# A two-layer decode step: compression units and conditioning moved ahead of the first norm, queries and keys projected first, the other projections mixed with attention

## The chip, the cores and the metric

The kernel runs on one core of one Trainium2 chip. The metric is the device time of one execution in microseconds (us). The engines are named as in the profile: PE is TensorE (PEld its weight loads), DVE is VectorE, ACT is ScalarE, POOL is GpSimd, and SP is SyncE, whose queue issues nearly all DMAs of this kernel, one after another and in a fixed order.

## The reference, cut to what matters

Two layers run over 256 prompt tokens and 8 sample tokens (264 columns in the kernel). Cut to what the change touches:

```python
def layer(x, c, ...):
    mod = silu(c) @ ada_w + ada_b                  # conditioning: 6 groups of 1024 columns
    sh1, sc1, g1, sh2, sc2, g2 = split(mod, 6)     # groups j = 0..5
    h = rmsnorm(x) * (1 + sc1) + sh1               # the first norm of a layer: groups 0 and 1
    q, kc, vc, ks, vs, kw, vw, gates, z, xbc, dt = split(h @ w_in, ...)
    kcmp = compress(cached pages of K ++ kc)       # 32-token blocks, stride 16, a small MLP with gelu
    vcmp = compress(cached pages of V ++ vc)
    o_cmp, p = compressed_attention(q, kcmp, vcmp)
    idx = top16(p);  o_slc = selected_blocks(q, idx, ks, vs)
    o_win = window_attention(q, kw, vw)
    o_att = sigmoid(gates) * (o_cmp, o_slc, o_win)
    xbc = silu(causal_conv4(xbc));  y = ssd(xbc, dt, state) * silu(z)   # Mamba-2 part
    x = x + g1 * (concat(o_att, rmsnorm(y)) @ w_out)
    h2 = rmsnorm(x) * (1 + sc2) + sh2
    return x + g2 * ((silu(causal_conv3(h2 @ w_gate)) * (h2 @ w_up)) @ w_down)
```

Every product is made in float32 accuracy out of two halves: ACT copies the high half of a weight tile (whi), DVE subtracts it for the low half (wlo), and TensorE adds high times high, high times low and low times high.

## The kernel before

A **projection tile** is one 128-column slice of w_in: a DMA of 512 KB into a staging buffer `st`, the split (whi on ACT, wlo on DVE), 24 matmuls of 264 columns into a `psmm` buffer, and an ACT copy out of it. A layer projects the gates and dt first (tile from in_wgd), then 6 **conv tiles** (x, B and C of the Mamba part: columns 10 to 15 of w_in, each followed by copies into xr, one ACT and three DVE steps on xa, a tanh and one DVE step into xc), then 10 **q/kv tiles** (keys and values 4 to 9, queries 0 to 3, and with 8 of them a fetch of four cached pages each). The 4 z tiles run inside attention.

**Conditioning** is the generator `ada(l, js)`. A group j is four steps; a step loads two tiles of 512 KB (`ada`, at the program's start `cpg`) and multiplies them in 8 matmuls into `psfl` (the trace counts 16 records). After a group come an ACT copy (adam), 2 transposes and a DVE add into `mod`. In the pools of attention two `ada` buffers exist, so one step's pair of tiles can be in flight: the pair's DMAs wait on SP until the matmuls of the step before have read the buffers, and what stands behind them in SP's queue waits too.

**Compression** of the cached pages is 8 units per layer (4 pairs of samples, keys and values). For each pair 16 DMAs bring pages of 128 KB (`cpg`; each needs a page number read from `pt`, the TENSOR_LOAD and ISA rows), the pages are split, and a unit has 48 matmuls of 252 columns into `pso` (weights cwh, cwl from in_cw), a gelu, and small matmuls.

The order of each engine's queue is static. A scheduler of the framework makes it from the program's order and its own durations; instructions issued while an engine's name is in `pinned` keep program order. Before, PINS is empty. Work is mixed by generators: `side` (conditioning) is advanced once a tile, `first` (the units) once a tile (EARLY, SX, SZ and SQ are all 1), and in attention the string SEQ advances S (samples), P (prompt), M (the Mamba part), B (selected blocks), Z (z tiles) and A (conditioning that is left, `fill`) one step a letter. In layer 0 the units run among the projection tiles. In layer 1 units and groups 0 and 1 have been done in the FFN of layer 0, and `rest` (groups 2 and 3 of layer 1) begins in its down-projection.

At the program's start (the last lines of the listing) two conditioning groups, the norm of layer 0 and the first unit come in this order. `together`, `square`, `norm` and `load` are small helpers; nearly all instructions are recorded with the line of one of them (L117), so groups are told apart by tile names.

Of the kernel before, what the change touches and what calls it, by code (L numbers as in the profile page):

```python
# [9 lines left out]
F32 = mybir.dt.float32  # L10
# [9 lines left out]
TP = 256  # L20
# [14 lines left out]
ADA_BUFS = {"cmp": 3, "att": 2, "ffn": 4}  # L35
# [63 lines left out]
CONSTS = _const_array()  # L99


@with_exitstack
def decode_step(ctx, tc, I, O):
# [75 lines left out]
    load(pt, I["pt"])  # L179
    cT = s1()[:, :256].rearrange("p (a b) -> p a b", a=KC)  # L180
# [131 lines left out]
    def ada(l, js, wide=0):  # L312
# [7 lines left out]
        for j in js:  # L320
            acc = fl()[:, :256]
            for kk in range(0, KC, 2):
                two = []
                if wide:
                    t = ph([2, 4, 256], "cpg", wide)
                    two = [(kk, t[:, 0]), (kk + 1, t[:, 1])]
                for k in (kk, kk + 1):
                    name = pools_names[-1]
                    if not wide:
                        t = sb([4, 256], "ada", ADA_BUFS[name[:3]], F32, pools[-2] if name == "attn1" else pools[-1])  # L330
                        two.append((k, t))
# [146 lines left out]
    def layer(l, A, pa, early, done, side, fill):  # L478
# [10 lines left out]
        for _ in range(GAP[l]):  # L489
            next(side, None)  # L490

        pb = begin(f"attn{l}") if early is None else None
# [27 lines left out]
        first = iter(()) if early is None else early()  # L520
# [45 lines left out]
        for m in range(6):  # L566
            if m % SX == 0:
                next(side, None)
            for _ in range(EARLY):
                next(first, None)  # L570
            o = mtile(I["win"][l, 10 + m], h)
            r = sb([291], "xr", 2)
            G.memset(r[:, 0:3], 0.0)
            G.tensor_copy(r[:, 259:291], cst_in[:, m, :])
            S.activation(r[:, 3:259], o[:, :TP], AF.Copy)
            S.activation(r[:, 262:291:4], o[:, TP:T], AF.Copy)
            G.tensor_copy(cout[:, m, :], r[:, 256:291])
            a = sb([288], "xa", 2)
            S.activation(a, r[:, 0:288], AF.Identity, scale=p["convh"][:, m, 0:1], bias=p["convh"][:, m, 4:5])
            for k in range(1, 4):  # L580
                V.scalar_tensor_tensor(a, r[:, k:k + 288], p["convh"][:, m, k:k + 1], a, op0=OP.mult, op1=OP.add)
            t = s1()
            S.activation(t, a, AF.Tanh)
            V.scalar_tensor_tensor(xc[:, m, :], t, 1.0, a, op0=OP.add, op1=OP.mult)
        store(O["conv"][l], cout)
# [19 lines left out]
        for m in list(range(4, 10)) + list(range(4)):  # L605
            if m % SQ == 0:
                next(side, None)
# [21 lines left out]
        run(first)  # L629
        run(side)  # L630
        if pb is None:
            done()
            pb = begin(f"attn{l}")
# [346 lines left out]
        spare = [slot(n, [KC, 128], F32R) for n in ("whi", "wlo")]  # L980
# [190 lines left out]
        pinned.update(PINS)  # L1171
# [94 lines left out]
    for k in range(KC - 1):  # L1266
        square(k)
    for _ in range(3):
        next(shift)
    load(cst, I["consts"])  # L1270
    square(KC - 1)
    run(shift)
    for _ in range(FIRST):
        next(units)
    params(1)
# [26 lines left out]
SEQ = ("ZBPPMASZPZMBMZZASPSZPPPPSPZAMMMBPSPPZMMAPMMBPPMMSAPBMSPMSASPMBZSMPSPMMSPSPMMPSPPPPPMPPPMPPPMSSSPMAMPAPPMMAPPMMSMP",) * 2  # L1302
CYCLE = "PMZSPAMPSMPBMZ"
GAP = (0, 0)
DOWN = 4
PINS = ()
FIRST, EARLY = 1, 1
SX, SZ, SQ = 1, 1, 1
# [126 lines left out]
```

## Time and profile before

| what | value |
|---|---|
| time, median of 3 runs | 1053.06 us (1047.99 to 1053.59) |
| profiled execution | 1040.78 us, its span 1039.0 us |
| busy: PE, DVE, ACT, POOL | 949.7, 650.7, 487.4, 167.8 us |
| share of PE in the span | 91% |
| chain that ended last | PE 76%, DMA 11%, DVE 7%, ACT 3% |
| mean DMA rate | 212 GB/s |

The span is one execution seen by the profiler. The program's parts stand in it as: the start to the first unit (0 to 42.6 us), the projections of layer 0 with the units (to 163.4), its attention (to 311.5), its output projection and FFN (to 593), the norm of layer 1 (to 609.6), its projections (to 670), its attention (to 816) and the rest. The marks are the starts of PE instructions.

### The profile page before, as it was taken

What the parts mean: (1) busy time and instruction counts of PE and PEld (TensorE: products, weight loads), DVE (VectorE), ACT (ScalarE), POOL (GpSimd) and SP (SyncE); (2) the same over time, 40 slices, a digit from 0 to 9 for tenths busy, and PEclk for the clock granted to TensorE, in tenths of its full rate; (3) what the DMA queues carried; (4) which work ended last, traced back from release to release, by engine and by line L of the source; (5) the groups of instructions that cost most, each with busy time, mean ns of one, the idle gap of its engine ahead of it and who ended that gap; (6) DMA issues with size and microseconds to landing.
All of it is one profiled execution on the core that took longest, in us unless ns stands there. A gap on an engine that the chain in (4) does not pass through costs nothing.

```text
span 1039.0 us, 21345 instructions
## 1 busy us (share of the span) xinstructions
PE 949.7 (91%) x7864; PEld 803.7 (77%) x7864; DVE 650.7 (63%) x1429; ACT 487.4 (47%) x1042; POOL 167.8 (16%) x337
## 2 busy tenths in 40 slices
PE   4599998988997998999999989998999799999996
PEld 2368997653585998999999868875447599999995
DVE  1386643867677665676754575485665687777553
ACT  1356543533444555555634344454244366666441
POOL 2000100225221101001101112031421221111110
PEclk9699999999997999999999989997599899999998
DMA  9987488246757786756675578725283835666651
GB/s 357 313 278 266 158 265 292 94 129 225 270 171 254 232 301 216 238 194 220 210 251 174 183 279 301 244 83 158 91 354 96 330 124 182 183 183 183 194 163 42
DMA packets 101258, 220.35 MB, mean 212 GB/s; under 512 B 11682, under 2 KB 54562, under 8 KB 101026
## 3 DMA queue, kind: packets, MB, share of 16 engines
q1 hardware_dynamic: 97058, 205.28, 59.8%
q0 software_dynamic: 3520, 13.17, 3.1%
q8 instruction: 62, 1.02, 0.4%
q10 hardware_dynamic: 576, 0.54, 0.2%
q14 instruction: 42, 0.34, 0.1%
HBM read 204.70 MB, written 14.25 MB: 211 GB/s over the span
## 4 chain that ended last, share of the span: by engine, by line
PE 76%; DMA 11%; DVE 7%; ACT 3%; issue 2%; SPq 1%; POOL 0%; DVEq 0%; ACTq 0%; POOLq 0%
PE psmm L117 40%; PE psat L117 22%; PE pso L117 10%; PE psfl L117 4%; DMA st<-in_cw_dram 3%; DMA ada<-in_ada_dram 3%; DVE wlo L117 2%; DMA cpg<-in_ada_dram 2%; DMA st<-in_wup_dram 1%; DMA page<-in_wst_dram 1%; DVE s L117 1%; SPq L117 1%; ACT whi L117 1%; DVE rs L117 1%; ACT psc L117 1%
## 5 line engine op out<-in xcount | busy, mean ns | idle before, releaser
L117 DVE TENSOR_TENSOR wlo<-st,whi 128x1024 fp32r<-128x1024 f32 (+1 forms) x204 | 232.7, 1142 | 152.6 <-ACT whi L117 149.1
L117 ACT ACTIVATE whi<-st 128x1024 fp32r<-128x1024 f32 (+1 forms) x204 | 201.6, 990 | 217.5 <-PE psmm L117 150.2
L117 PE MATMUL psmm<-hhi,whi 128*128 128x264 f32 x800 | 233.7, 293 | 3.3 <-ACT whi L117 1.4
L117 PE MATMUL psmm<-hhi,wlo 128*128 128x264 f32 x800 | 228.5, 286 | 1.1 <-DVE wlo L117 1.1
L117 PE MATMUL psmm<-hlo,whi 128*128 128x264 f32 x800 | 228.2, 286 | 0.0
L117 PEld LDWEIGHTS psmm<-hhi,whi 128*128 128x128 f32 x800 | 151.4, 189 | 17.0 <-ACT whi L117 5.2
L117 PEld LDWEIGHTS psmm<-hhi,wlo 128*128 128x128 f32 x800 | 150.9, 189 | 5.2 <-DVE wlo L117 2.4
L117 PEld LDWEIGHTS psmm<-hlo,whi 128*128 128x128 f32 x800 | 151.5, 190 | 2.4 <-issue 2.0
L117 PE MATMUL psmm<-act,whi 128*128 128x264 f32 x704 | 128.5, 284 | 0.0
L117 PEld LDWEIGHTS psmm<-act,whi 128*128 128x128 f32 x704 | 108.9, 188 | 1.6 <-issue 1.6
L117 PE MATMUL psat<-hhi,whi 128*128 128x264 f32 x352 | 100.8, 286 | 2.2 <-ACT whi L117 2.2
L117 PE MATMUL psat<-hhi,wlo 128*128 128x264 f32 x352 | 100.5, 286 | 1.0 <-DVE wlo L117 1.0
L117 PE MATMUL psat<-hlo,whi 128*128 128x264 f32 x352 | 100.6, 286 | 0.0
L117 PE MATMUL psmm<-act,wlo 128*128 128x264 f32 x352 | 99.9, 284 | 0.0
L117 PE MATMUL pso<-whi,cwh 128*128 128x252 f32 x256 | 74.8, 292 | 8.7 <-ACT whi L117 8.0
L117 PE MATMUL pso<-wlo,cwh 128*128 128x252 f32 x256 | 74.1, 290 | 1.8 <-DVE wlo L117 1.8
L117 PE MATMUL pso<-whi,cwl 128*128 128x252 f32 x256 | 73.6, 287 | 0.0
L117 PEld LDWEIGHTS psat<-hhi,whi 128*128 128x128 f32 x352 | 67.1, 191 | 2.5 <-ACT whi L117 2.5
L117 POOL COPY fout<-xr 128x26 f32<-128x26 f32 x44 | 28.1, 639 | 247.0 <-ACT xr L117 247.0
L117 PEld LDWEIGHTS psat<-hhi,wlo 128*128 128x128 f32 x352 | 66.7, 190 | 1.2 <-DVE wlo L117 1.2
L117 PEld LDWEIGHTS psat<-hlo,whi 128*128 128x128 f32 x352 | 67.2, 191 | 0.0
L117 PEld LDWEIGHTS psmm<-act,wlo 128*128 128x128 f32 x352 | 66.1, 188 | 0.0
(305 smaller groups left out, 1579.5 us busy)
## 6 DMA issues: line engine op xcount, KB each, us to landing
st<-in_wup_dram SPq DMA_DIRECT2D x88, 512.0 KB, 3.9
ada<-in_ada_dram SPq DMA_DIRECT2D x80, 512.0 KB, 5.2
st<-in_wdn_dram SPq DMA_DIRECT2D x44, 512.0 KB, 3.6
st<-in_win_dram SPq DMA_DIRECT2D x40, 512.0 KB, 4.9
page<-in_slcc_dram SPq DMA_DIRECT2D x128, 128.0 KB, 2.7
cpg<-in_ada_dram SPq DMA_DIRECT2D x16, 512.0 KB, 9.4
st<-in_cw_dram SPq DMA_DIRECT2D x16, 512.0 KB, 5.9
cpg<-in_cmpc_dram SPq DMA_DIRECT2D x64, 128.0 KB, 3.7
```

The source lines that it names most:

```text
L117: ins = f(*a, **k)
```

## The change

- **Start.** The first 129 columns of the constants are loaded at once, the others after the third unit. All 8 units of layer 0 come before its first norm, with one conditioning step (groups 0 and 1) after each, in program order on PE and SP; PE's pin ends after the conditioning, SP's at the fourth q/kv tile. The x tile is loaded after the first unit's pages. Conditioning at the start uses 9 `ada` buffers rather than 4 pairs of `cpg` ones.
- **Projections.** The 10 q/kv tiles follow the gates. The conv tiles become a generator that runs when attention's generators exist: after each conv tile a few steps of P, B and S (strings EARLY). SEQ loses the steps that stand there; its later part is the same. (pp, in the rows below, are the prompt's probabilities of compressed attention, a step of P.)
- **Conditioning.** Layer 0: group 2 at the side of the q/kv tiles, 3 and 4 in attention (before: 2 and 3, then 4). Layer 1: the side gets `rest` and then group 3, which `rest` already holds (groups 2 and 3), so that group is computed twice; group 4 goes to attention (before: `rest` and group 4 at the side).
- The buffers `spare` are taken after the conv tiles. The rest is renaming and removed arguments.

```diff
-ADA_BUFS = {"cmp": 3, "att": 2, "ffn": 4}
+ADA_BUFS = {"cmp": 9, "att": 2, "ffn": 4}
...
+CST0 = CONST_W["one"][0] + 1
...
     load(pt, I["pt"])
+    load(cst[:, :CST0], I["consts"][:, :CST0])
     cT = s1()[:, :256].rearrange("p (a b) -> p a b", a=KC)
...
-    def ada(l, js, wide=0):
+    def ada(l, js):
...
-                if wide:
-                    t = ph([2, 4, 256], "cpg", wide)
-                    two = [(kk, t[:, 0]), (kk + 1, t[:, 1])]
                 for k in (kk, kk + 1):
                     name = pools_names[-1]
-                    if not wide:
-                        t = sb([4, 256], "ada", ADA_BUFS[name[:3]], F32, pools[-2] if name == "attn1" else pools[-1])
-                        two.append((k, t))
-                    load(two[k - kk][1], I["ada"][l, j, k])
+                    t = sb([4, 256], "ada", ADA_BUFS[name[:3]], F32, pools[-2] if name[:4] == "attn" else pools[-1])
+                    load(t, I["ada"][l, j, k])
+                    two.append((k, t))
...
-        for m in range(6):
-            if m % SX == 0:
-                next(side, None)
-            for _ in range(EARLY):
-                next(first, None)
-            o = mtile(I["win"][l, 10 + m], h)
...
+        def convolved():
+
+            for m in range(6):
+                o = mtile(I["win"][l, 10 + m], h)
...
+                yield
+            store(O["conv"][l], cout)
...
         for m in list(range(4, 10)) + list(range(4)):
-            if m % SQ == 0:
-                next(side, None)
-            for _ in range(EARLY):
-                next(first, None)
-            if pb is not None and len(ring) < PAGES:
+            next(side, None)
+            if len(ring) < PAGES:
                 fetch()
             o = mtile(I["win"][l, m], h)
+            if m == 7:
+                pinned.clear()
...
-        pinned.update(PINS)
+        for m, _ in enumerate(convolved()):
+            for c in EARLY[m] if m < 6 else ():
+                next(bg[c], None)
+        spare += [slot(n, [KC, 128], F32R) for n in ("whi", "wlo")]
         for c in SEQ[l]:
             next(bg[c], None)
...
     params(0)
+    params(1)
+    p0 = begin("cmp0")
+    units, shift = compress(0, 1, 4), ada(0, (0, 1))
+    pinned.update(PINS)
+    for i in range(8):
+        next(units)
+        if i == 0:
+            load(x, I["xT"])
+        if i == 2:
+            load(cst[:, CST0:], I["consts"][:, CST0:])
+            for k in range(KC):
+                square(k)
+        next(shift, None)
+    run(shift)
+    pinned.discard("PE")
+    run(units)
+    end(p0)
     pa = begin("att0")
-    A = pools[-1]
-    p0 = begin("cmp0")
-    units = compress(0, 1, 4)
-    load(x, I["xT"])
-    shift = ada(0, (0, 1), 4)
...
-    rest = layer(0, A, pa, lambda: units, lambda: end(p0), ada(0, (2, 3)), [ada(0, (4,))])
+    rest = layer(0, pools[-1], pa, ada(0, (2,)), [ada(0, (3, 4))])
     pa = begin("att1")
-    layer(1, pools[-1], pa, None, lambda: None, chain(rest, ada(1, (4,))), [])
+    layer(1, pools[-1], pa, chain(rest, ada(1, (3,))), [ada(1, (4,))])
...
-SEQ = ("ZBPPMASZPZMBMZZASPSZPPPPSPZAMMMBPSPPZMMAPMMBPPMMSAPBMSPMSASPMBZSMPSPMMSPSPMMPSPPPPPMPPPMPPPMSSSPMAMPAPPMMAPPMMSMP",) * 2
+SEQ = ("ZMAZZMMZZAZZAMMMSPZMMAPMMPPMMSAPMSPMSASPMBZSMPSPMMSPSPMMPSPPPPPMPPPMPPPMSSSPMAMPAPPMMAPPMMSMP",) * 2
...
-PINS = ()
-FIRST, EARLY = 1, 1
-SX, SZ, SQ = 1, 1, 1
+EARLY = ("PBS", "PPBS", "PPBS", "PPS", "PPB", "PPB")
+PINS = ("PE", "SP")
```

SP at the program's start, before (cst: constants, s: the conditioning vector from cT, par: parameters, cpg from in_ada: conditioning tiles, st from in_cw: compression weights, cpg from in_cmpc: pages):

```order
L117 DMA pt<-in_pt_dram 1x64
L117 DMA s_2_64<-in_cT_dram 128x256
L117 DMA par_76<-in_par_dram 128x288
L117 DMA x_66<-in_xT_dram 128x2112
L117 DMA adab_112<-in_adab_dram 128x48
L117 DMA cpg_115<-in_ada_dram 128x1024 x2
...
L117 DMA cst_61<-in_consts_dram 128x1581
L117 DMA cpg_154<-in_ada_dram 128x1024 x2
...
L117 DMA st_230<-in_cw_dram 128x1024
L299 TENSOR_LOAD pt
```

And now:

```order
L118 DMA pt<-in_pt_dram 1x64
L118 DMA cst_61<-in_consts_dram 128x129
L118 DMA s_2_65<-in_cT_dram 128x256
L118 DMA par_77<-in_par_dram 128x288
L118 DMA par_84<-in_par_dram 128x288
L118 DMA st_98<-in_cw_dram 128x1024
L118 DMA st_102<-in_cw_dram 128x1024
L301 TENSOR_LOAD pt
```

The first pages come behind 7 loads instead of 24 (the conditioning pairs count as two); x, adab and the first conditioning tiles come behind the first pair's 16 pages.

SP in the projections of layer 1, before: from one conditioning pair to the third behind it (page from in_slcc: cached pages of the selected branch; st from in_win: q/kv tiles):

```order
L117 DMA ada_7920<-in_ada_dram 128x1024
L117 DMA ada_7922<-in_ada_dram 128x1024
L299 TENSOR_LOAD pt
...
L117 DMA page_8206<-in_slcc_dram 128x256
L117 DMA st_8221<-in_win_dram 128x1024
L117 DMA ada_7977<-in_ada_dram 128x1024
L117 DMA ada_7979<-in_ada_dram 128x1024
...
L117 DMA page_8252<-in_slcc_dram 128x256
L117 DMA st_8267<-in_win_dram 128x1024
L117 DMA ada_8038<-in_ada_dram 128x1024
```

And now:

```order
L118 DMA ada_7936<-in_ada_dram 128x1024
L118 DMA ada_7938<-in_ada_dram 128x1024
L118 DMA st_8021<-in_win_dram 128x1024
...
L118 DMA page_8064<-in_slcc_dram 128x256
L118 DMA ada_7994<-in_ada_dram 128x1024
L118 DMA ada_7996<-in_ada_dram 128x1024
...
L118 DMA page_8064<-in_slcc_dram 128x256
L118 DMA st_8079<-in_win_dram 128x1024
L118 DMA ada_8052<-in_ada_dram 128x1024
```

In both one w_in tile stands between two pairs. On PE the four steps that these pairs feed were 47 to 49 matmuls (two tiles) apart and are now 16 to 22 (two thirds of a tile to nearly one) apart; they end in the eighth of the ten q/kv tiles. The group that they belong to is the second group 3; before it was group 4.

DVE at the start of attention in layer 0, before (wlo: a tile's low half; qz, psc, pm: the first scores of P and S; xa, xc: the conv steps):

```order
L117 TENSOR_TENSOR wlo_1820<-st_1817,whi_1819 128x1024
L117 TENSOR_TENSOR wlo_1852<-st_1849,whi_1851 128x1024
L117 TENSOR_TENSOR wlo_1901<-st_1902,whi_1900 128x1024
L117 COPY qz_72<-q_1449 64x4x4 x4
L117 SCALAR_TENSOR_TENSOR psc_1935<-cst_61,psat_1937 128x384
L117 SCALAR_TENSOR_TENSOR psc_1935<-cst_61,psat_1938 128x384
L117 COPY cum_1961<-psat_1959 128x16
L117 TENSOR_REDUCE pm_280_1945<-psc_1935 128x6
```

And now:

```order
L118 TENSOR_TENSOR wlo_1893<-st_1890,whi_1892 128x1024
L118 SCALAR_TENSOR_TENSOR psc_1740<-cst_61,psat_1742 128x384
L118 SCALAR_TENSOR_TENSOR psc_1740<-cst_61,psat_1743 128x384
L118 SCALAR_TENSOR_TENSOR xa_1732<-xr_1726,halfw_79,xa_1732 128x288
L118 TENSOR_REDUCE pm_239_1750<-psc_1740 128x6
L118 SCALAR_TENSOR_TENSOR xa_1732<-xr_1726,halfw_79,xa_1732 128x288
L118 TENSOR_TENSOR pm_239_1750<-pm_239_1750 128x2
L118 SCALAR_TENSOR_TENSOR xa_1732<-xr_1726,halfw_79,xa_1732 128x288
L118 TENSOR_SCALAR psm_1741<-pm_239_1750 128x2x2
L118 SCALAR_TENSOR_TENSOR xc_1188<-s_234_1737,xa_1732 128x288
```

The conv tile's four DVE steps now stand between the steps of a softmax; the same holds for all six conv tiles of a layer.

## Rows read from the trace of the kernel before

**Rows 1.** The page, its part 1: busy us (share of the span) xinstructions.

```profile
PE 949.7 (91%) x7864; PEld 803.7 (77%) x7864; DVE 650.7 (63%) x1429; ACT 487.4 (47%) x1042; POOL 167.8 (16%) x337
```

**Rows 2.** Four stretches: us, busy us (x count) by engine, PEclk, DMA share, GB/s.

```profile
0.00:42.60 42.60, 17.28 (x148) 7.01 (x148) 8.96 (x31) 9.77 (x21) 5.81 (x15) 0.82 0.91 332
42.60:163.40 120.80, 117.59 (x994) 104.85 (x995) 72.14 (x140) 62.20 (x129) 9.02 (x24) 0.98 0.76 254
...
593.00:609.60 16.60, 11.40 (x88) 5.68 (x87) 11.41 (x39) 5.53 (x13) 0.35 (x2) 0.79 0.76 259
609.60:670.00 60.40, 58.10 (x511) 52.99 (x510) 32.77 (x65) 29.37 (x59) 9.88 (x21) 1.00 0.87 303
```

**Rows 3.** SP at the start: start us, us in the queue, engine, line, DMA.

```profile
2.52 0.43 SPq L117 DMA_DIRECT2D adab<-in_adab_dram  x1
...
21.85 0.90 SPq L117 DMA_DIRECT2D st<-in_cw_dram  x2
25.98 13.64 SPq L117 DMA_DIRECT2D cpg<-in_cmpc_dram  x16
...
60.64 0.38 SPq L117 DMA_DIRECT2D st<-in_win_dram  x1
...
61.84 10.74 SPq L117 DMA_DIRECT2D cpg<-in_cmpc_dram  x16
```

**Rows 4.** PE, first unit: start, us, op [idle before <-releaser]; the clock then.

```profile
42.62 0.58 PE L117 MATMUL pso<-whi,cwh 128*128 128x252 f32 x1 [8.03 <-ACT whi L117]
...
42.60:47.60 5.00, 4.50 (x19) 4.21 (x20) 2.31 (x6) 1.00 (x2) 0.37 (x2) 0.50 0.95 318
```

**Rows 5.** PE in layer 0's projections: steps, unit transposes; eight tiles alone.

```profile
71.27 1.07 PE L117 MATMUL psfl<-ada,cs 128*32 128x256 f32 x16
...
78.12 0.69 PE L117 MATMUL psat<-w2h,hid 128*63 128x64 f32 x8
...
88.69 0.44 PE L117 MATMUL psat<-hid,w2h 128*64 128x126 f32 x4
...
139.80:162.60 22.80, 22.80 (x191) 22.80 (x190) 8.58 (x7) 9.15 (x15) 0.55 (x1) 1.00 0.88 290
```

**Rows 6.** PE timeline, norm of layer 1: its sums, a conditioning step, the first tile.

```profile
593.03 0.60 PE L117 MATMUL psat<-row,cst 128*1 128x264 f32 x2
...
607.04 1.07 PE L117 MATMUL psfl<-ada,cs 128*32 128x256 f32 x16 [0.75 <-DMA ada<-in_ada_dram]
...
608.93 0.39 PE L117 MATMUL psmm<-hhi,whi 128*128 128x264 f32 x1
```

**Rows 7.** Conditioning tiles, 585 to 665 us: who waited, and landing; the SP timeline.

```profile
  PE psfl L117: 2.6, 3
...
DMA to landing us min/median/max: 3.6/4.8/7.2
...
616.50 0.81 SPq L117 DMA_DIRECT2D ada<-in_ada_dram  x2
```

**Rows 8.** Two stretches of attention, up to pp; columns as in rows 2.

```profile
163.40:223.70 60.30, 53.08 (x535) 38.66 (x534) 38.02 (x113) 27.06 (x88) 11.59 (x27) 0.97 0.45 150
670.00:720.80 50.80, 44.90 (x454) 33.88 (x453) 37.06 (x108) 25.17 (x81) 12.24 (x27) 0.96 0.31 97
```

**Rows 9.** PE timeline there: waits for a conditioning tile and for pp.

```profile
177.32 1.03 PE L117 MATMUL psfl<-ada,cs 128*32 128x256 f32 x8 [2.00 <-DMA ada<-in_ada_dram]
...
720.82 0.39 PE L117 MATMUL psat<-cst,pp 128*15 128x128 f32 x1 [3.68 <-DVE pp L117]
```

**Rows 10.** DVE, 60 to 160 us, groups: busy us, mean ns | idle before.

```profile
L117 DVE TENSOR_TENSOR wlo<-st,whi 128x1024 fp32r<-128x1024 f32 x17 | 20.8, 1225 | 18.0 <-ACT whi L117 14.7 <-DMA page<-in_slcc_dram 1.7 <-DMA st<-in_cw_dram 1.7
...
L117 DVE SCALAR_TENSOR_TENSOR xa<-xr,halfw,xa 128x288 f32<-128x288 f32 x18 | 9.3, 517 | 0.4
...
L117 DVE SCALAR_TENSOR_TENSOR xc<-s,xa 128x288 f32<-128x288 f32 x6 | 2.8, 463 | 3.1 <-ACT s L117 3.1
```

**Rows 11.** A stretch of the FFN in layer 0; columns as in rows 2.

```profile
400.00:420.00 20.00, 16.79 (x132) 15.47 (x131) 14.10 (x25) 12.36 (x25) 2.91 (x6) 0.91 0.70 226
```

More of the change, by code (lines that the diff above doesn't have):

```diff
@@ L476, in mtile, with layer @@
         return out
-    def layer(l, A, pa, early, done, side, fill):
+    def layer(l, A, pa, side, fill):
         p = PAR[l]
@@ L488, in layer @@
         h = (hhi, hlo)
-        for _ in range(GAP[l]):
-            next(side, None)
-        pb = begin(f"attn{l}") if early is None else None
+        pb = begin(f"attn{l}")
         def slot(tag, shape, dt=F32):
@@ L517, in fetch @@
                 ring.append((v[:, :, 0, :], v[:, :, 1, :]))
-        first = iter(()) if early is None else early()
         w = sb([KC, 32], "st", WB[2])
@@ L565, in layer @@
         xc = pha([6, 288], "xc", 1)
-        for m in range(6):
-            if m % SX == 0:
-                next(side, None)
-            for _ in range(EARLY):
-                next(first, None)
-            o = mtile(I["win"][l, 10 + m], h)
[L572 to L585, printed above, removed]
+        def convolved():
+            for m in range(6):
+                o = mtile(I["win"][l, 10 + m], h)
+                r = sb([291], "xr", 2)
+                G.memset(r[:, 0:3], 0.0)
+                G.tensor_copy(r[:, 259:291], cst_in[:, m, :])
+                S.activation(r[:, 3:259], o[:, :TP], AF.Copy)
+                S.activation(r[:, 262:291:4], o[:, TP:T], AF.Copy)
+                G.tensor_copy(cout[:, m, :], r[:, 256:291])
+                a = sb([288], "xa", 2)
+                S.activation(a, r[:, 0:288], AF.Identity, scale=p["convh"][:, m, 0:1], bias=p["convh"][:, m, 4:5])
+                for k in range(1, 4):
+                    V.scalar_tensor_tensor(a, r[:, k:k + 288], p["convh"][:, m, k:k + 1], a, op0=OP.mult, op1=OP.add)
+                t = s1()
+                S.activation(t, a, AF.Tanh)
+                V.scalar_tensor_tensor(xc[:, m, :], t, 1.0, a, op0=OP.add, op1=OP.mult)
+                yield
+            store(O["conv"][l], cout)
         zz = pha([4, T], "zz", 1)
@@ L605, in layer @@
         for m in list(range(4, 10)) + list(range(4)):
-            if m % SQ == 0:
-                next(side, None)
-            for _ in range(EARLY):
-                next(first, None)
-            if pb is not None and len(ring) < PAGES:
+            next(side, None)
+            if len(ring) < PAGES:
                 fetch()
             o = mtile(I["win"][l, m], h)
+            if m == 7:
+                pinned.clear()
             if m < 4:
@@ L628, in layer @@
             S.activation(vn[:8, b], o[:8, 256:384], AF.Copy)
-        run(first)
         run(side)
-        if pb is None:
-            done()
-            pb = begin(f"attn{l}")
         def samples():
@@ L979, in layer @@
         y = ph([4, T], "y", 1)
-        spare = [slot(n, [KC, 128], F32R) for n in ("whi", "wlo")]
+        spare = []
         outs = []
@@ L1259, in decode_step @@
     params(0)
-    pa = begin("att0")
-    A = pools[-1]
-    p0 = begin("cmp0")
-    units = compress(0, 1, 4)
-    load(x, I["xT"])
-    shift = ada(0, (0, 1), 4)
[L1266 to L1275, printed above, removed]
-    rest = layer(0, A, pa, lambda: units, lambda: end(p0), ada(0, (2, 3)), [ada(0, (4,))])
+    params(1)
[15 more added lines that the diff above has]
+    end(p0)
+    pa = begin("att0")
+    rest = layer(0, pools[-1], pa, ada(0, (2,)), [ada(0, (3, 4))])
     pa = begin("att1")
-    layer(1, pools[-1], pa, None, lambda: None, chain(rest, ada(1, (4,))), [])
+    layer(1, pools[-1], pa, chain(rest, ada(1, (3,))), [ada(1, (4,))])
     rs, = inv_roots(SUMS[-1], 1, 1.0 / D)
@@ L1301 @@
 WAITS = (0, 0, 0, 1, 1)
-SEQ = ("ZBPPMASZPZMBMZZASPSZPPPPSPZAMMMBPSPPZMMAPMMBPPMMSAPBMSPMSASPMBZSMPSPMMSPSPMMPSPPPPPMPPPMPPPMSSSPMAMPAPPMMAPPMMSMP",) * 2
+SEQ = ("ZMAZZMMZZAZZAMMMSPZMMAPMMPPMMSAPMSPMSASPMBZSMPSPMMSPSPMMPSPPPPPMPPPMPPPMSSSPMAMPAPPMMAPPMMSMP",) * 2
 CYCLE = "PMZSPAMPSMPBMZ"
-GAP = (0, 0)
 DOWN = 4
-PINS = ()
-FIRST, EARLY = 1, 1
-SX, SZ, SQ = 1, 1, 1
+EARLY = ("PBS", "PPBS", "PPBS", "PPS", "PPB", "PPB")
+PINS = ("PE", "SP")
 RATE = (1, 1, 2, 1)
```

## The prediction

> **What bounds the kernel now.** I read the page's busy times first: PE works 91% of the span, so what counts is its work and the few places where it stands still [rows 1]. The table of stretches says where those are [rows 2]. From 0 to 42.6 us PE is busy for 17.3 of 42.6; in the two projection stretches for 117.6 of 120.8 and 58.1 of 60.4; around the norm of layer 1 for 11.4 of 16.6. The start is a matter of SP's queue: the first pages are issued at 25.98, behind 8 MB of conditioning tiles and 1 MB of weights, their 16 issues last until 39.62, and the first unit starts at 42.62 [rows 3, 4], 3.0 us after the last issue. In attention PE idles 7.2 of 60.3 us in layer 0 and 5.9 of 50.8 in layer 1 up to the step on pp [rows 8]; two named waits there are 2.00 us for a conditioning tile and 3.68 us for pp [rows 9]. So three things can change: when work starts, how long the projection stretches wait, and how much of the attention's idle time is filled. A difference within 0.5% (about 5 us) is what a measurement of this kernel can't tell from no change.
>
> **Layer 0, start to attention.** Before, the mark is 163.4 us. After:
> - First unit. Seven loads stand ahead of the first page. Five loads end at 2.95 us, some 0.45 apart [rows 3], so the seventh ends at 3.9. From a load to the first page it takes 0.8 us (61.02 to 61.84) or 3.2 (22.75 to 25.98), and sixteen pages take 10.74 or 13.64 [rows 3]; I take the middles, 2.0 and 12.2, as nothing tells which the new start resembles. With 3.0 us for the last page's landing and split the first unit starts at 21.1.
> - Four pairs. From 71.27 to 88.69 lie two units, two steps of 1.07, small matmuls of 0.69 and one tile: 17.42 us. A tile alone is 24 x 22.8/191 = 2.86 [rows 5]. So a unit is (17.42 - 2.14 - 0.69 - 2.86)/2 = 5.87, and a pair with its two steps and its small matmuls (0.69 and 0.44) is 15.0; four are 60.0. The clock stood at .50 (1.2 GHz, the lower of its two levels) for 5 us from the first unit's start on, after 8 us in which PE stood still [rows 4]: 2.5 lost. Later pages hide: a second batch would be in by 36, the unit needs it at 38.6. If that cover went, a pair would cost its batch of pages, 10.74 to 13.64 and 3 us for its loads, about the same. Conditioning ends with 0.8 us of adam and transposes: 84.4.
> - The norm was hidden by units and isn't any more. Layer 1 shows its price bare: 593.03, the sums, to 608.93, the first tile, 15.9 us, with the gates and a step in it [rows 6]. First tile at 100.3.
> - Ten q/kv tiles 28.6, three steps 3.2, transposes 1.0, and the waits of the **ring**: only one step's pair of tiles is in flight, so from the end of one step to the next there must lie the two issues (0.9; 0.81 in [rows 7]) and the landing, 4.8 at the median [rows 7], together 5.7. Between the four steps PE has 3.9 us (gates and a tile), 2.86 and 2.86, so it waits 1.8 + 2.8 + 2.8 = 7.5. That gives 140.6.
> - Left for later are six conv tiles (17.2) and the four steps and transposes of group 3 (4.7). 140.6 + 21.9 = 162.5: **-0.9 us**. The start that was gained is spent on a bare norm and a ring. Bounds: the low prices of the first pages and a landing of 3.6 give -7, the high ones and 6.0 give +5.
>
> **Layer 1, norm to attention.** Group 3 is computed twice: 4 x 1.07 + 0.4 = +4.7 us of PE work [rows 5]. There is no doubt of that term, since PE is full. The ring: before, two tiles lay between steps, and PE waited 2.6 us in all for conditioning [rows 7]. After, five gaps between steps are shorter than 5.7: 4.65, 4.9, 2.15, 2.5 and 3.1 us of PE work (1.6 tiles; 1.4 tiles and transposes; 18, 16 and 22 matmuls with their transposes or scores), so it waits 1.0 + 0.8 + 3.6 + 3.2 + 2.6 = 11.2, which is +8.6. The w_in tiles are queued behind those pairs on SP, one between two pairs, and come once a ring period too, so nothing else fills the wait. Sum **+13.3** (+7.9 with a landing of 3.6, +20 with 6.0).
>
> **Attention.** The idle time that conv tiles can fill is 7.2 + 5.9 = 13.1 us [rows 8]. But a conv tile asks DVE for 1.225 + 3 x 0.517 + 0.463 = 3.24 us [rows 10] against 2.86 of PE, and DVE is already busy 38.0 of the 60.3 and 37.1 of the 50.8 us [rows 8]; the longest wait there ends with DVE's pp [rows 9], and the conv steps now stand between the softmax's steps on DVE. From all filled (-13.1) to nothing filled and DVE's surplus, 6 x 0.38 = 2.3 in each layer, on top (+4.6). I take the half, **-6.5**: ScalarE's and the ring's waits can be filled, DVE's not.
>
> **The clock** I set at nothing. In a stretch of the FFN with 3.2 us of idle time in 20 the granted clock is .91, a mixture of 2.4 and 1.2 GHz [rows 11], and the thinned projections have about as large a share of idle time. But a tile that runs slower between two steps shortens the wait behind it, since the ring's period stays. The Trainium skill (page "TensorE: Matmul & The Clock Gate", section "HAM oscillation — how this bites in real kernels") speaks against this change more strongly: matmul bursts that take turns with waits for DMA can start again and again at the low clock. By that rule the sum would be that of the fourth rival below; here the rows agree only as far as the .91.
>
> **Sum:** -0.9 + 13.3 - 6.5 = +5.9, in the profiled execution 1040.78 + 5.9 = 1046.7. The median of the runs stands at 1053.06/1040.78 = 1.0118 of it: **1059.0 us**.
>
> **Rivals.**
> 1. *The loads land sooner.* The price of the ring is the landing; 3.6 us is the least of this stretch [rows 7], and SP, held up by the ring, issues fewer loads that could crowd it. Against it: the DMA share there is .87 [rows 2], and as many steps go through in less time. At 3.6 a gap needs 4.5: layer 0 waits 3.9, layer 1 5.8, 9.7 instead of 18.7, so 9.0 less. 1040.8 + 5.9 - 9.0 = 1037.7, so 1049.9: not slower. It decides from a landing of about 4.2. The Trainium skill (page "DMA: Bandwidth & Descriptors", section "Anatomy of one DMA — SWDGE (gpsimd) path") gives a fit, for another issuing engine, of 2.0 us and the bytes by 436 GB/s, an estimate of 3.2 us for 512 KB; by it the ring would wait 7.2 us instead of 18.7 and the time come to 1047.4. The trace's least and median are above it.
> 2. *PE waits for nothing but what is left of the ring:* as 1, and conv tiles fill all of attention's idle time too, 6.6 more. 1031.1, so 1043: faster. For it: conv tiles have no inputs but what is already there. Against it: DVE, as above.
> 3. *The loads land later.* Twice the conditioning in less time: at 6.0, half-way to the longest landing of 7.2 [rows 7], each of three gaps in layer 0 and six in layer 1 costs 1.2 more: +10.8, 1057.5, so 1070.
> 4. *The low clock* holds over the seven tiles between steps (three in layer 0, four in layer 1): each takes twice its 2.86, +20, if nothing of it comes off the waits: 1066.7, so 1079.
> That the change doesn't do what it says can be left out: the order shows the units first and the conv tiles late.
>
> **How the numbers follow.** Forecast .40, rival 1 .17, rival 2 .20, rival 3 .16, rival 4 .07. The forecast's time is 1059. Range: rival 2's time at the low end, 1043, where half of it lies below; rival 3's and a little more at the high end, 1073. Left out are half of rival 2 and rival 4, under .2. Faster by over 0.5% (below 1047.8): rival 2 and a part of rival 1, .24. Slower by over 0.5% (above 1058.3): rivals 3 and 4 and somewhat over half of the forecast, .46. Within: .30.
>
> **What would show it.** In the profile of the changed kernel: the first unit's matmul near 21 us; psmm of the first q/kv tile near 100, which is step by step the claim on the bare norm; waits of PE's psfl for conditioning tiles of 5 to 10 us in each layer's projections (below 4, rival 1; above 12, rival 3); four steps (64 records of psfl) more in layer 1 than before; a clock there of .90 or more, or else rival 4. In attention: PE's idle time up to pp, together 6 to 7 us instead of 13; if it is near nothing, rival 2, and if pp's wait grows, my half was too kind. Wrong altogether I would be if the pages' batches didn't come in time and the units stood waiting for them, or if the start's pinned order held up DVE or ACT.

## The result

The changed kernel takes 1097.21 us (median of 4 runs, 1092.62 to 1100.66) against 1050.53 for the kernel before: a ratio of 1.0517, with a 95% interval of 1.0465 to 1.0568. It is slower by some 5%. The forecast was 1059 in a range of 1043 to 1073: the sign was right, the size far off. Each ratio in this document leaves out runs that lie over 1.5% above the fastest of the same kernel. The profiled execution has a span of 1090.8 us, 51.8 more than before.

The page of the changed kernel, its first part, to be held against [rows 1] (columns as there):

```profile
span 1090.8 us, 21470 instructions
...
PE 964.2 (88%) x7930; PEld 818.6 (75%) x7930; DVE 659.9 (60%) x1430; ACT 489.1 (45%) x1043; POOL 162.9 (15%) x337
```

TensorE does 14.5 us more and stands still 37.3 us longer (126.6 instead of 89.3). Of the 14.5 only 4.7 are the group computed twice; the rest is the same work at a lower clock (.936 over the whole span, .945 before). Between equal points of the program the 51.8 us are spread so: up to the step on pp in layer 0 +23.2 (223.7 to 246.9), from there to the sums of the second norm +7.7 (315.9 to 346.7; two conditioning steps, 2.1 us, fall behind pp now and none did before), to the gates of layer 1 +0.8, from its first gates matmul to pp there +23.7 (118.2 to 141.9), and the rest -3.5. (The 311.5 us that stand above as the end of attention in the kernel before are the end of its output projection; neither argument nor sums use that mark.)

The windows of the changed kernel from the start to the end of the q/kv tiles in layer 0 (columns as in rows 2; [rows 2, 4] answer to them):

```profile
0.00:18.00 18.00, 0.00 (x0) 0.00 (x0) 5.85 (x14) 6.16 (x9) 0.95 (x8) 1.00 0.75 221
18.00:47.70 29.70, 24.87 (x188) 22.56 (x188) 12.68 (x21) 11.31 (x22) 0.00 (x0) 0.94 0.91 323
47.70:57.67 9.97, 0.00 (x1) 0.00 (x1) 3.03 (x5) 4.77 (x13) 5.45 (x7) 0.65 0.84 274
57.67:99.60 41.93, 41.09 (x372) 33.96 (x372) 14.57 (x30) 15.38 (x36) 0.48 (x3) 0.96 0.53 176
99.60:112.00 12.40, 7.94 (x56) 5.20 (x56) 8.91 (x34) 3.70 (x11) 0.00 (x0) 0.60 0.09 11
112.00:163.30 51.30, 42.78 (x320) 37.30 (x320) 18.31 (x34) 17.86 (x32) 0.69 (x1) 0.90 0.85 293
...
113.58:163.30 49.72, 41.20 (x308) 36.74 (x308) 17.27 (x32) 16.47 (x29) 0.69 (x1) 0.90 0.85 289
```

Row by row: the units start at 18.0; after three of them PE does nothing for ten us; the other five run nearly without a gap. Then comes the bare norm, in which the DMA engines move 11 GB/s: SP stands still. The last 1.6 us of the gates run into the row from 112.00; the first q/kv tile begins at 113.58, and the ten tiles take 49.7 us with 8.5 idle, at a clock of .90, a mixture of 2.4 and 1.2 GHz.

**The ten us in the start.** PE, ACT and POOL timelines of the changed kernel:

```profile
30.37 0.58 PE L118 MATMUL pso<-whi,cwh 128*128 128x252 f32 x1 [2.68 <-ACT hid L118]
...
57.67 1.04 PE L118 MATMUL psat<-row,cst 128*1 128x264 f32 x2 [9.97 <-POOL row L118]
```

```profile
26.58 1.06 ACT L118 ACTIVATE cwh<-st 128x1024 fp32r<-128x1024 f32 x1 [7.59 <-DMA st<-in_cw_dram]
...
50.04 0.63 ACT L118 ACTIVATE whi<-cpg 128x512 fp32r<-128x512 f32 x1 [2.45 <-DMA cpg<-in_cmpc_dram]
...
51.14 1.03 ACT L118 ACTIVATE s<-x 128x264 f32<-128x264 f32 x3
```

```profile
51.69 0.63 POOL L118 COPY row<-s 128x264 f32<-128x264 f32 x1 [50.20 <-ACT s L118]
52.40 5.21 POOL L118 TENSOR_TENSOR row<-row,s 128x264 f32<-128x264 f32 x6
```

The sums of the first norm (psat<-row) are pinned on PE behind the third unit. They need the squares, which on ACT stand behind a page's split that waits for its DMA until 50.04, and then seven steps of POOL one after another, until 57.6. Nothing may overtake them on PE. The second unit's wait of 2.68 us has another cause: ACT's read of the first unit's result stands behind the splits of the second compression weights, for whose load ACT waited 7.59 us.

**SP in the norm and the q/kv tiles.** The SP timeline of the changed kernel:

```profile
90.14 0.85 SPq L118 DMA_DIRECT2D ada<-in_ada_dram  x2
91.53 1.90 SPq L118 DMA_DIRECT2D page<-in_slcc_dram  x4
93.48 0.42 SPq L118 DMA_DIRECT2D st<-in_win_dram  x1
110.04 1.18 SPq L118 DMA_DIRECT2D ada<-in_ada_dram  x2
111.76 1.90 SPq L118 DMA_DIRECT2D page<-in_slcc_dram  x4
113.71 0.42 SPq L118 DMA_DIRECT2D st<-in_win_dram  x1
114.66 0.85 SPq L118 DMA_DIRECT2D page<-in_slcc_dram  x2
118.36 0.82 SPq L118 DMA_DIRECT2D ada<-in_ada_dram  x2
```

One w_in tile is issued at 93.48, the next at 113.71: between them a conditioning pair waits 16 us for the step before it, which runs with the gates, after the norm. In the ten tiles PE waits so (columns: who <- for whom: us in total, times, longest):

```profile
PE psmm L118 <- ACT whi L118: 5.2, 3, 2.5
PE psmm L118 <- DVE wlo L118: 2.0, 3, 0.8
```

On PE the second q/kv tile then waits twice, for its high and its low half, and runs slowly (timeline, and the clock in the windows of two tiles and of a later stretch):

```profile
117.66 1.07 PE L118 MATMUL psfl<-ada,cs 128*32 128x256 f32 x16
121.03 0.39 PE L118 MATMUL psmm<-hhi,whi 128*128 128x264 f32 x1 [2.30 <-ACT whi L118]
...
122.29 0.48 PE L118 MATMUL psmm<-hhi,wlo 128*128 128x264 f32 x1 [0.75 <-DVE wlo L118]
```

```profile
121.00:127.00 6.00, 5.22 (x32) 4.78 (x36) 1.23 (x1) 0.19 (x1) 0.00 (x0) 0.72 0.75 275
137.00:144.00 7.00, 6.32 (x29) 5.77 (x30) 2.33 (x2) 1.45 (x2) 0.00 (x0) 0.58 0.89 291
147.00:153.00 6.00, 5.76 (x47) 5.44 (x46) 1.65 (x3) 3.19 (x6) 0.69 (x1) 1.00 0.78 281
```

The step at 117.66 did not wait; the tile behind it did. Six us at .72 held 32 matmuls, and seven at .58 held 29, where six at 1.00 held 47.

### The profile page after: what moved, and what is told of

Read it like the earlier page. It is cut to its first block, busy times and chain, and to the rows that moved or that the text cites. A ratio compares the mean times of both kernels' runs of the same rounds, so it can differ in the third digit from the quotient of the medians.

```text
span 1090.8 us, 21470 instructions
## 1 busy us (share of the span) xinstructions
PE 964.2 (88%) x7930; PEld 818.6 (75%) x7930; DVE 659.9 (60%) x1430; ACT 489.1 (45%) x1043; POOL 162.9 (15%) x337
## 4 chain that ended last, share of the span: by engine, by line
PE 61%; DMA 8%; DVE 7%; SPq 3%; ACT 3%; issue 2%; POOL 0%; ACTq 0%; DVEq 0%; POOLq 0%
PE psmm L118 35%; PE psat L118 19%; PE pso L118 4%; SPq L118 3%; PE psfl L118 3%; DVE wlo L118 2%; DMA ada<-in_ada_dram 2%; DMA st<-in_wup_dram 2%; DMA st<-in_win_dram 2%; ACT whi L118 1%; ACT psc L118 1%; DMA cpg<-in_cmpc_dram 1%; DMA page<-in_slcc_dram 1%; DVE rs L118 1%; DVE pm L118 1%
## 5 line engine op out<-in xcount | busy, mean ns | idle before, releaser
L118 PE MATMUL psmm<-hhi,whi 128*128 128x264 f32 x800 | 237.8, 298 | 11.8 <-ACT whi L118 10.4
L118 PE MATMUL psmm<-hhi,wlo 128*128 128x264 f32 x800 | 233.6, 293 | 7.5 <-DVE wlo L118 7.4
L118 PE MATMUL psmm<-hlo,whi 128*128 128x264 f32 x800 | 231.7, 290 | 0.0
L118 PEld LDWEIGHTS psmm<-hhi,whi 128*128 128x128 f32 x800 | 154.7, 194 | 30.1 <-ACT whi L118 17.9
L118 PEld LDWEIGHTS psmm<-hhi,wlo 128*128 128x128 f32 x800 | 154.2, 193 | 11.3 <-DVE wlo L118 9.9
L118 PEld LDWEIGHTS psmm<-hlo,whi 128*128 128x128 f32 x800 | 155.0, 194 | 1.7 <-issue 1.4
L118 PEld LDWEIGHTS pso<-whi,cwh 128*128 128x128 f32 x256 | 52.0, 203 | 26.0 <-ACT whi L118 18.4
L118 DVE SCALAR_TENSOR_TENSOR xa<-xr,halfw,xa 128x280 f32<-128x280 f32 (+1 forms) x124 | 63.7, 514 | 6.9 <-ACT xa L118 5.0
```

The lines of the kernel that those rows point to most:

```text
L118: ins = f(*a, **k)
```

## The experiments

Ratios are to the kernel before, measured on the same chip in the same job, with the 95% interval; the changed kernel's own is 1.0517. Spans and windows are of the profiled executions.

### The group computed twice: nodup

```diff
-    layer(1, pools[-1], pa, chain(rest, ada(1, (3,))), [ada(1, (4,))])
+    layer(1, pools[-1], pa, rest, [ada(1, (4,))])
```

> The changed kernel without the second computation of group 3 in layer 1 (the side of the q/kv tiles gets only the rest of groups 2 and 3). Theory (start, ring and repeated group each cost their part): the four steps, 4.7 us of TensorE work, and most of the waits for late weight tiles between them (7.0 us in layer 1's projections) go, and some low clock with them: 12 to 18 us less than the changed kernel, about 1082. Rival (mixing the conv tiles with attention is what costs): only the 4.7 us of work go, about 1092.

Measured: 1.0382 (1.0321 to 1.0443), 1.35% or 14 us less, as the theory had it. In the trace layer 1 takes 129.2 us from the gates to pp instead of 141.9, 12.7 less. The doubled group costs its 4.7 us of work and 8.0 more in its ring: 6.2 of idle time and 1.8 of busy time. The window of the changed kernel (that of nodup stands further down):

```profile
634.24:776.15 141.91, 122.07 (x1083) 96.91 (x1078) 75.34 (x188) 57.60 (x148) 18.19 (x48) 0.94 0.56 192
```

### The sums of the first norm: late, sumslate

```diff
         if i == 2:
             load(cst[:, CST0:], I["consts"][:, CST0:])
+        if i == 5:
             for k in range(KC):
                 square(k)
```

> The changed kernel with the squares of x issued after the sixth unit instead of the third, so that the sums of the first norm don't stand in the pinned TensorE order ahead of data that come late. Theory: the wait of 10.0 us for the sums at 47.7 goes, but the third pair's pages are in only near 54, so about half of it comes back as a wait for pages: 4 to 7 us less, about 1091. Rival (the sums alone held up the units): all 10 us go, 1087. Rival (pages alone): nothing changes, 1097.

Measured: 1.0497 (1.0456 to 1.0538), no difference that the intervals tell. But not for the reason of any of the three theories. The two largest waits of PE between 18 and 99 us in this kernel, behind that for the first unit (columns as above):

```profile
PE psat L118 <- POOL kcp L118: 7.3, 1, 7.3
PE pso L118 <- ACT hid L118: 6.1, 2, 3.3
```

The first ends at 79.7 us with the sums (psat<-row; kcp is what POOL does right behind the seven steps). The wait only moved to the new place of the sums, since squares and sums were moved together. So they were parted: seven squares after the third unit, the last and the sums after the sixth.

```diff
-            for k in range(KC):
+            for k in range(KC - 1):
                 square(k)
+        if i == 5:
+            square(KC - 1)
```

> The changed kernel with the squares of x still issued after the third unit, but the two matmuls that sum them over partitions only after the sixth. Theory: the wait of 7 to 10 us is the price of pinned TensorE order (the sums stand ahead of units that could run, while ScalarE's squares and GpSimd's seven additions, some 6 us one after another, are made); with the sums placed later the units go on. But the third pair's pages land only at 50 to 55 us, so the fourth unit starts near 55 instead of 61: conditioning ends 4 to 7 us sooner, and the time falls from 1.052 of the kernel before to about 1.047. Rival (the pages are the limit): no change.

Measured: 1.0488 (1.0383 to 1.0593), too wide to tell 5 us. The trace tells more: the ten-us wait is gone, three waits for units' inputs (5.5 us in all) stay, and the gates begin at 98.75 instead of 107.25:

```profile
98.75 0.65 PE L118 MATMUL psmm<-hhi,st 128*32 128x264 f32 x1 [1.39 <-ACT hhi L118]
```

The same row of the changed kernel:

```profile
107.25 1.49 PE L118 MATMUL psmm<-hhi,st 128*32 128x264 f32 x5 [1.39 <-ACT hhi L118]
```

### Half of the change: startonly, startsum, convfirst

startonly is the kernel before with the changed program start in place of its own, and its layers as they were:

```diff
+    units, shift = compress(0, 1, 4), ada(0, (0, 1))
+    pinned.update(PINS)
+    for i in range(8):
...
-    rest = layer(0, A, pa, lambda: units, lambda: end(p0), ada(0, (2, 3)), [ada(0, (4,))])
+    rest = layer(0, pools[-1], pa, None, lambda: None, ada(0, (2, 3)), [ada(0, (4,))])
...
```

> The kernel before with the new start only: units and conditioning ahead of the norm of layer 0 in pinned order; projections, side work and attention in both layers as before. Theory: conditioning ends near 100 us, the first tile comes near 112, then 16 tiles (46 us), 8 steps (8.6) and some 8 us of waits: attention of layer 0 starts near 176 instead of 163.4, so 10 to 16 us more than before, 1060 to 1067. Rival (the start is neutral and mixing costs): 1048 to 1055.

Measured: 1.0242 (1.0180 to 1.0304), some 25 us, more than either theory had. Its layer 0 has the eight steps of groups 2 and 3 beside 16 tiles with no units among them, and waits there for weight tiles (8.6 us) as the changed kernel does:

```profile
PE psmm L118 <- ACT whi L118: 5.0, 4, 1.3
PE psmm L118 <- DVE wlo L118: 3.6, 4, 1.4
```

With the sums parted as above (startsum):

> The run named startonly with the sums of the first norm behind the sixth unit: layers as in the kernel before, with groups 2 and 3 beside the projections of layer 0. Theory: 5 to 9 us less than startonly, 1.016 to 1.02; what stays are eight steps of the ring beside layer 0's 16 tiles, which were hidden among units before. Rival (the start alone is to blame): 1.00 to 1.005, as the run named best.

Measured: 1.0102 (1.0013 to 1.0190), 1.4% less than startonly, more than the theory's 5 to 9 us and short of its rival's 1.00 to 1.005; in the traces the gates begin 7.0 us sooner (98.8 instead of 105.8), and from there to pp both take 136 us.

convfirst keeps start and doubled group, undoes the mixing and gives attention the string of before:

```diff
+        for _ in convolved():
+            next(side, None)
         for m in list(range(4, 10)) + list(range(4)):
             next(side, None)
...
-        for m, _ in enumerate(convolved()):
-            for c in EARLY[m] if m < 6 else ():
-                next(bg[c], None)
...
```

> The changed kernel with the mixing undone: conv tiles right after the gates and ahead of the q/kv tiles, conditioning at their side too, attention with the string of before. Start and repeated group stay. Theory (start, ring, repeated group): the ring has 16 tiles to spread over instead of 10, so 8 to 15 us less in the two projection stretches, and up to 7 us more in attention: 1085 to 1097. Rival (mixing is what costs): 25 us less or more than that, 1072 or below.

Measured: 1.0189 (1.0152 to 1.0226), 34 us less than the changed kernel: more than the theory's 8 to 15, and what its rival (mixing) had. But two things are undone at once here, as the conv tiles give the ring 16 tiles to lie among. The next runs part them.

### Ring and mixing, each with and without the other: noside, convapart, apartnoside

noside takes the conditioning from beside the q/kv tiles (and computes group 3 of layer 1 once):

```diff
-    rest = layer(0, pools[-1], pa, ada(0, (2,)), [ada(0, (3, 4))])
+    rest = layer(0, pools[-1], pa, iter(()), [ada(0, (2, 3, 4))])
...
-    layer(1, pools[-1], pa, chain(rest, ada(1, (3,))), [ada(1, (4,))])
+    layer(1, pools[-1], pa, iter(()), [rest, ada(1, (4,))])
```

> The changed kernel with no conditioning at the side of the q/kv tiles in either layer: groups 2 to 4 of layer 0 and the rest of groups 2 and 3 and group 4 of layer 1 all go to the steps A of attention; group 3 of layer 1 is computed once. Conv tiles stay mixed with attention. Theory (the ring: one step in flight, weight tiles queued on SP behind a pair that waits): the q/kv stretches lose their waits and low clock, 8 us in layer 0 and 12 in layer 1, and 4.7 us of doubled work: 1.052 falls to about 1.03, and part of it may come back as waits for conditioning in attention (2 to 5 us). Rival (mixing conv tiles with attention is what costs): only the doubled work goes, 1.047.

convapart leaves the conv tiles behind the q/kv tiles but puts no attention steps between them, and gives attention the string of before:

```diff
-        for m, _ in enumerate(convolved()):
-            for c in EARLY[m] if m < 6 else ():
-                next(bg[c], None)
+        for _ in convolved():
+            pass
...
```

> The changed kernel with the conv tiles where it has them, behind the q/kv tiles, but as six tiles without attention steps between; attention takes the string of before. Ring, start and doubled group stay. Theory (ring): q/kv stretches as in the changed kernel, conv tiles back to back, attention as before: 1.052 falls by at most 5 to 8 us, 1.045 or more. Rival (mixing): falls by 20 us or more, to 1.03 or below, as with the conv tiles put first.

apartnoside does both:

> The changed kernel without conditioning beside the q/kv tiles (all of it that is left goes to the steps A of attention, group 3 of layer 1 once) and with the six conv tiles as a block behind the q/kv tiles instead of mixed with attention steps. The start is that of the changed kernel. Theory (ring, doubled group and mixing are the whole loss behind the start): 1.00 to 1.015 of the kernel before. Rival (conv tiles that come late cost by their place alone): 1.02 or more.

Measured:

| start of the changed kernel, and | conditioning beside the q/kv tiles, group 3 twice | conditioning in attention, once |
|---|---|---|
| conv tiles mixed with attention | 1.0517 (the changed kernel) | 1.0237 (1.0159 to 1.0315) |
| conv tiles as a block | 1.0342 (1.0242 to 1.0442) | 1.0030 (0.9991 to 1.0068) |

Within the intervals the two add: the ring with the doubled group costs 2.8 to 3.1%, mixing 1.75 to 2.1%, whichever way one goes through the table, and what is left is 0.3% against the kernel before. That kernel pays for a ring of its own, though: against oldstart (below), which has none either, the start (with the wait for its sums) and the late conv tiles still cost 1.0%. For noside and convapart neither theory had the whole: I had held the ring for the whole loss behind the start, and its rival the mixing. The forecast for apartnoside, with both, held. Undoing the mixing also gives attention its order of steps of before; the two were not tested apart.

How mixing costs is seen in layer 0 between gates and pp, without the ring. noside, mixed (windows; the second is 155 to 175 us, among the conv tiles), and its largest waits of PE:

```profile
105.44:231.69 126.25, 116.00 (x996) 94.71 (x996) 78.99 (x189) 59.65 (x149) 18.47 (x48) 0.91 0.53 175
155.00:175.00 20.00, 17.61 (x140) 13.51 (x140) 12.86 (x35) 9.92 (x27) 5.61 (x14) 0.67 0.49 158
```

```profile
PE pso L118 <- ACT pT L118: 3.0, 2, 1.6
PE psat L118 <- POOL s L118: 2.7, 2, 2.0
PE psmm L118 <- ACT hhi L118: 2.0, 2, 1.4
PE psmm L118 <- DVE wlo L118: 1.4, 2, 1.2
```

apartnoside, as a block:

```profile
105.83:218.53 112.70, 109.02 (x995) 90.46 (x995) 77.96 (x189) 59.46 (x150) 19.95 (x48) 0.96 0.58 197
155.00:175.00 20.00, 19.16 (x202) 16.38 (x201) 14.86 (x39) 11.05 (x32) 4.52 (x16) 1.00 0.45 143
```

```profile
PE psmm L118 <- ACT hhi L118: 2.0, 2, 1.4
PE pso L118 <- ACT pT L118: 1.5, 1, 1.5
PE psat L118 <- POOL s L118: 0.8, 1, 0.8
```

The same 996 matmuls take 126.3 or 112.7 us: 6.6 of the difference are idle time (10.3 and 3.7), 7.0 are busy time at a lower clock. Among the mixed conv tiles short waits for scores and halves of tiles follow one another (2.0 us just before the 20 us of the second window, then 0.4, 1.2 and 0.8), and the clock stands at .67 over these 20 us. In layer 1 the same pair of kernels takes 120.6 and 112.3 us.

### The pinned order: nopin

```diff
-PINS = ("PE", "SP")
+PINS = ()
```

> The changed kernel with nothing pinned: the scheduler is free to order TensorE and SP at the start. Theory (the pinned order makes the wait for the sums): the wait goes and units and norm may overlap, 6 to 12 us less, 1.04 to 1.046. Rival (the order that the scheduler finds is worse): 1.055 or more, with waits for conditioning tiles that come behind pages on SP.

Measured: 1.0366 (1.0293 to 1.0439), 15 us less, more than the theory's 6 to 12. In its trace the wait for the sums is 3.6 us instead of 10.0, the gates begin at 104.1, 3 us sooner, and from there to pp layer 0 takes 133.4 us instead of 139.6, with SP too free in the first q/kv tiles. That is 9 us. The rest of that trace doesn't show more: its layer 1 takes 146.4 us from the gates to pp, 4.5 more than the changed kernel's, and its span is only 3.5 us shorter, since it is the slowest execution of the four. Where the other 6 us by ratio lie stays open.

### What is left of the start: best, best2, best3, oldstart

best keeps the new start with the sums parted, puts the conv tiles first without mixing and computes group 3 once. best2 takes in addition all conditioning from beside the projections, as noside does. best3 is best2 with the conv tiles as a block behind the q/kv tiles. oldstart is the kernel before with noside's edit only.

> The new start kept, all else mended: conv tiles ahead of the q/kv tiles, attention's string of before, group 3 of layer 1 computed once, the sums of the first norm behind the sixth unit. Theory: the start still costs the bare norm and some low clock in layer 0, about 5 to 10 us against the kernel before; the rest is gone: 1.005 to 1.01. Rival (the start is a gain once its waits are gone): 0.99 or below.

> As the run named best (new start with the sums later, conv tiles first, attention's string of before), but all conditioning that is left goes to attention instead of standing beside the projection tiles. Theory (ring): the projections lose their last waits, 4 to 8 us, attention gets twelve steps more and waits for their loads: 0.995 to 1.01. If the ring with 16 tiles around it still cost much, below 0.99.

> The run named best2 once more, on the same chip as the run with the old start, to set them side by side: 0.985 to 0.995 of the kernel before by the first run; equal to the run with the old start within 0.5% if the start is neutral, 1% less if the start is a gain.

> As best2, but with the six conv tiles as a block behind the ten q/kv tiles instead of ahead of them, still not mixed with attention. Theory (place is indifferent, mixing costs): as best2 within 0.5%. Rival (late conv tiles cost by their place): 1% more.

> The kernel before, with its own start and order of projections, but without conditioning beside the projection tiles: groups 2 to 4 of layer 0 and the rest of 2 and 3 and group 4 of layer 1 go to the steps A of attention. Theory (the new start is about neutral, what the run named best2 gained is the ring's): 0.985 to 0.995 of the kernel before, as best2. Rival (the new start is a gain of its own, about 1%): 0.995 to 1.005.

| kernel | ratio to before | interval |
|---|---|---|
| best | 0.9994 | 0.9946 to 1.0041 |
| best2 | 0.9888 | 0.9813 to 0.9963 |
| best2again: best2 on the chip of oldstart | 0.9888 | 0.9824 to 0.9952 |
| best3 | 0.9952 | 0.9885 to 1.0019 |
| oldstart | 0.9928 | 0.9890 to 0.9965 |

best was forecast at 1.005 to 1.01 and came out level. best2 beats both kernels, the kernel before by 1.1%: 1033.27 us. Its forecast was 0.995 to 1.01; below 0.99 was the sign that a ring with 16 tiles around it still costs much. oldstart beats them too, the kernel before by 0.7% with an edit of two lines, as forecast: that gain is of a projection stretch without the ring. Side by side, the new start with the sums parted and the old start differ by 0.4%, inside their intervals: no gain of the new start is shown, and no loss. Whether the late place of the conv tiles costs by itself (best3 against best2, 0.6%) the intervals don't tell; best3's ratio rests on four of its ten runs, which go from 1031 to 1051 us. best3 and apartnoside differ in the sums alone: 0.9952 and 1.0030, some 8 us, with intervals that overlap, which agrees with the 8.5 us in the trace of sumslate.

Layer 1, gates to pp, where three kernels do the same 1017 or 1018 matmuls, shows what ring and mixing together cost beside the idle time. Before, nodup (mixed, ring among 10 tiles) and best (not mixed, ring among 16 tiles), a window of each:

```profile
602.62:720.82 118.20, 108.62 (x1017) 89.29 (x1013) 75.11 (x187) 57.64 (x148) 22.11 (x48) 0.98 0.63 212
```

```profile
638.12:767.33 129.21, 115.53 (x1018) 93.65 (x1013) 75.41 (x187) 57.37 (x147) 18.67 (x48) 0.94 0.52 179
```

```profile
607.79:721.56 113.77, 107.26 (x1018) 88.96 (x1013) 75.44 (x187) 57.41 (x148) 22.28 (x48) 0.99 0.61 207
```

Of the 11.0 us between nodup and the kernel before, 4.1 are idle time and 6.9 busy time at .94 instead of .98.

## Why the prediction was right in sign and wrong in size

The span grew by 51.8 us, the forecast was 5.9. Of the 45.9 between them 13.3 arise before the first q/kv tile (113.6 us instead of 100.3), 9.4 in the ten q/kv tiles (49.7 instead of 40.3), 12.7 from there to the second norm (183.4, where the forecast's terms give 170.8), 13.3 in layer 1 from the gates to pp (141.9 instead of 118.2 + 13.3 - 2.9), and the rest is -2.7. Step by step:

- **First unit.** Forecast 21.1, measured 18.0: both unknown prices fell at their lower ends (16 pages in 10.15 us, the first some 1 us after the last load).
- **Four pairs.** The unit's price held (5.9 us), but from the first unit to the end of the conditioning it took 81.6 us instead of 63.3, 15.6 of them idle. The steps that failed are "Later pages hide" and the place of the norm's sums. The second batch of pages was issued from 22.65 to 36.83, not by 33, the second pair of compression weights came late, which I had not priced at all, and PE waited 2.7 and 2.0 us before the second and third units. And the sums of the norm, which I had put behind the units as part of the bare norm, stood in the pinned order behind the third and cost 10.0 us. Conditioning ended at 99.6 instead of 84.4. In the trace of sumslate 8.5 of these 15 us go with the sums. That the start's pinned order would hold up an engine the prediction had named as a sign of being wrong; it was PE, and not DVE or ACT.
- **Bare norm.** With the sums made early it took from 99.6 to the first tile at 113.6, 14.0 us instead of 15.9. Right in kind.
- **Ring, layer 0.** I put 7.5 us of waits and PE waited 7.8 (5.2 for whi, 2.0 for wlo, 0.6 for adam). The place was different: the steps did not wait, the tiles behind them did, because SP issued their weights only after the pair in front. So the sign that I had set, PE's wait for conditioning tiles, stood at nothing in this stretch, which was to mean rival 1, and the time was lost all the same. The landings, on which I had hung two rivals, were shorter than before (3.5, 4.0 and 6.3 us at least, median and most, where [rows 7] had 3.6, 4.8 and 7.2), and PE waited no less. What I missed was the clock: PE was busy 41.2 us in that stretch, where the forecast had 28.6 + 3.2 + 1.0 = 32.8.
- **Layer 1.** The forecast of 4.7 us for the doubled group and some 9 for its ring is near what nodup measured (14 us by ratio, 12.7 in the trace): the size was right. The place was not, as in layer 0: up to pp PE waited 2.5 us for conditioning tiles and 8.9 for halves of weight tiles. The 23.7 us by which this stretch grew are 4.7 of doubled work, 10.3 of idle time and 8.7 of busy time at a lower clock, for which the forecast had nothing.
- **Attention.** The step that failed is the sign of -6.5: conv tiles were to fill half of the idle time. Mixing measured +1.75 to +2.1%, some 18 to 22 us in two layers. I had weighed DVE's load only. The conv tiles are themselves chains (load, whi, wlo, matmuls, xr, xa, xc), and in a static queue each of their waits holds up the softmax behind it and the other way round. That each chain holds up the other is read from the static order and from noside's waits, which are of both kinds (halves of tiles, and pT and s of attention); no run shows it by itself. The idle time up to pp did not fall by half: it is 7.6 us between 163.3 and 246.9 in layer 0 and 9.4 between 693.2 and 776.2 in layer 1, 17.0 together, where [rows 8] has 7.2 and 5.9. The waits for pp are gone, and others stand in their place.
- **Clock.** "At nothing" was wrong by some 10 us. The argument was that a slower tile shortens the wait behind it. It fails since the low clock stays on for tiles that have no wait behind them (137 to 144 us at .58) and for the attention steps (.91 from gates to pp in noside's layer 0, which has no ring there). The fourth rival had it, at .07 and for the q/kv tiles alone. The Trainium skill's page "TensorE: Matmul & The Clock Gate", section "HAM oscillation — how this bites in real kernels", which I cited and set aside, was the better guide: bursts that take turns with waits ran at .58 to .72 here.

Of the 51.8 us about 37 are idle time, 5 are doubled work and 10 are clock, by the page's first part; where the waits were undone, both came back together (apartnoside against noside, best against nodup).

## What to carry to other kernels

Filling idle time with other work did not pay here, since that work had waits of its own; in a static queue two interleaved chains can wait for each other, so try a block of ready work next to a chain before putting it piece by piece into it. A load that waits for a buffer holds up what stands behind it in its queue (here SP issued nothing for 16 us), so look in the order for what stands behind such a load, above all before a stretch in which its consumer can't run yet. And price a stretch with many short waits at the clock that a stretch like it shows, not at full clock.

## What of the hardware was not expected

Waits far shorter than I had thought harmful went with a low clock: in the changed kernel waits of 2.30 and 0.75 us, 6 us at .72; in the mixed conv tiles waits of 0.4 to 2.0 us, 20 us at .67. The ten us in which PE did nothing at all (47.70 to 57.67) left no more behind: after them came 4.3 us at .62 and then the higher level of 2.4 GHz. Windows of the changed kernel:

```profile
57.67:62.00 4.33, 4.33 (x27) 1.99 (x28) 0.42 (x1) 0.00 (x0) 0.00 (x0) 0.62 1.00 354
62.00:99.60 37.60, 36.76 (x348) 31.97 (x346) 14.15 (x29) 15.38 (x36) 0.48 (x3) 1.00 0.47 155
```

As an estimate from these rows, 4.33 us at .62 and 6 us at .72 each lose 1.6 to 1.7 us against full clock: here a wait of two or three us cost as much clock as one of ten.
